# A layer of three branches on one core: half of one branch's projection moved ahead, and two branches of the merge in turn

## The chip, the cores and the metric

The kernel runs on one core of a Trainium2 chip. The metric is the device time of one execution in microseconds (us); three runs of the kernel before gave 1663.97, 1666.6 and 1668.9 us, with a median of 1666.6.

## What is computed

One layer of a flow-matching backbone works on 1024 latent tokens of width 1024 (and 256 context tokens). Three branches of width 512 run on one input projection: 0, a Hyena branch of two long convolutions; 1, a two-dimensional transform in groups of channels; 2, a bidirectional mLSTM. The part of the reference that the change touches merges them:

```python
ys = jnp.stack([y_hy, y_fn, y_ml], axis=2)
proj = jnp.einsum("blkc,kcd->blkd", ys, lp["w_branch"])
g = jax.nn.sigmoid(gate_pre).reshape(B, L, N_BRANCH, D_MODEL)
return jnp.sum(g * proj, axis=2) @ lp["w_out"]
```

A mixture-of-experts part and a final norm follow. Everything is float32.

## The kernel before

All is held with channels on the 128 partitions and the 1024 tokens along a row. A float32 product is made of three: both operands are split into a high part, rounded by a cast on ScalarE (ACT), and the low rest, a subtraction on VectorE (DVE) or GpSimd (POOL) (`split`, L213; `parts`, L223), and `mm3` (L228) multiplies high by high, high by low and low by high into one PSUM tile. Loads go through SyncE's queue (SP) (`load`, L218).

The order of the parts: the input projection, the mLSTM and the transform branch, whose results lie in DRAM (`yd[2]`, `yd[1]`) long before they are used; the last gates (`gate`, L830; the last one by `proj_last`, L766, whose evacuations, `rest`, come in the next stage); the Hyena convolutions (`stage_conv`, L1144); the merge (`stage_merge`, L1509); the output projection (`stage_out`, L1552).

The convolutions run in four passes (order and half of the channels; L1158), each of eight blocks j (even or odd frequencies `par`, part `fb`). A block takes a forward product into a bank of PSUM tag `gp` (two), multiplies it with the filter `kk` on VectorE (L1057, L1059), splits the result, and, two blocks later, adds the inverse product to the tiles `acc` (`conv_inv`, L1062): four per half pass, six banks in all. `conv_in` (L993) makes the next pass's input by transposes; `conv_out` (L1096) makes a pass's output, and in passes 2 and 3 sends it from the tiles `f` to `yd[0]`. Matrices come through `mat` (L969) and four buffers `ms`. At the start, `rest` is ordered behind the cast of the last of three forward matrices (L1155).

The merge runs over the branches 2, 1, 0 (n = 0, 1, 2; L1521). For each it loads four y tiles of 128x1024 through two buffers (`GA` `y`) and splits them, then makes eight groups d: a weight block of 128x512 (split by ACT and POOL, three buffers), a gate tile `g`, 24 products (two halves of 512 tokens, four parts k, three products each) into `pb` (four tiles, all eight banks), and VectorE's gate multiplication; from n = 1 on, POOL adds to `acc`. Branch 1 prepares the parts of `w_out` beside its groups. Branch 1's y tiles have a place of their own, GY; those of branches 2 and 0 share one (`y0` to `y3` in GN and G, one buffer each).

What sets the order: each engine runs its instructions in an order that a scheduler draws up when the program is built, from the order of the source, its priorities and its idea of the durations; it may put an instruction whose operands come later behind another. Tiles live in pools that are laid out like stacks from two sides of SBUF, so that a new pool lies where closed ones were, and a tile waits for the tiles that lay in its place. On the left side T (18 tiles of 4 KB, the projection's input) and then P (`w`, three of 4 KB, `wh`, `wl` and `z`, two of 4 KB each, in this order) are followed by C1 (56 KB) and CN (24 KB), and these by MT, WO and GN (112 KB). On the right, CA, C and CT (24, 48 and 20 KB) are followed by GA, G, GT and GY, of which GY (32 KB) covers CT and the last output's tiles `u` and `f` in it, and some tiles of C.

Of the kernel before, what the change touches and what calls it, by code (L numbers as in the profile page):

```python
# [8 lines left out]
F32 = mybir.dt.float32  # L9
F32R = mybir.dt.float32r  # L10
I32 = mybir.dt.int32
AF = mybir.ActivationFunctionType
ALU = mybir.AluOpType
# [4 lines left out]
L = 1024  # L18
# [146 lines left out]
class Prog:  # L165
# [22 lines left out]
        self.n += 1  # L188
        return self.dp.tile(list(shape), dt, name=f"{name}_{self.n}", tag=f"{name}_{self.n}")

    PSB = {"gp": 2, "q": 2, "b1": 2, "pb": 1, "acc": 6, "ph": 8}

    def ps(self, tag="pb", shape=(128, 1024)):
        self.n += 1
        pool = self.pg if tag == "gp" else self.pp
        return pool.tile(list(shape), F32, name=f"{tag}_{self.n}", tag=tag, bufs=self.PSB[tag])

    def psum(self, name):
# [4 lines left out]
        if name != "start":  # L203
            self.PSB = dict(self.PSB, pb=3)
        if name == "merge":
            self.pgc.__exit__(None, None, None)
        if name in ("merge", "moe"):
            self.PSB = dict(self.PSB, pb=4)
        self.ppc = self.tc.tile_pool(name=name, bufs=1, space=PSUM, reuse_waits="tile")
# [924 lines left out]
    def conv_first(self):  # L1134
# [6 lines left out]
        for kind in "fi":  # L1141
            self.mat(kind, 0, 0, 0)

    def stage_conv(self):  # L1144
        nc = self.nc
        self.pool("C1")
        self.pool("CN")
        self.psum("conv")
        blocks = [(par, fb) for par in range(2) for fb in range(4)]
        passes = [(o, half) for o in range(2) for half in range(2)]  # L1150
        ut, last, acc = {0: self.ut0}, [], {}
        for fb in (1, 2, 3):
            self.mat("f", 0, 0, fb)
        first = self.copied, self.lower
        with self.tc.issue_after(self.copied.ins):  # L1155
            for f in self.rest:
                f()
        for n, (o, half) in enumerate(passes):  # L1158
            acc[n] = {}
            for j, (par, fb) in enumerate(blocks):  # L1160
                for kind, i in (("f", j + FA), ("i", j - IA)):
                    if n == 0 and 0 <= i < 4:
                        self.mat(kind, 0, 0, i)
                if n == 0 and j < 4:
                    for k in range(2):
                        self.mat("o", 1, k, j)
                with ExitStack() as es:
                    for i in () if n or j else first:
                        es.enter_context(self.tc.issue_after(i.ins))
                    y = self.conv_fwd(ut[n], o, half, par, fb)  # L1170
                if len(last) == 2:
                    self.conv_inv(*last.pop(0))
                if j == 1 and n:
                    out = self.conv_out(acc[n - 1], *passes[n - 1])
                if n and j in (1, JA, JB):
                    next(out, None)
                last.append((acc[n], y, o, half, par, fb))
                if j == JC and n < 3:
                    ut[n + 1] = list(self.conv_in(self.xd[0], passes[n + 1][1], *((self.out_tiles,) if n else ())))
        for a in last:  # L1180
            self.conv_inv(*a)
        for _ in self.conv_out(acc[3], 1, 1):
            pass
        self.psum("merge")
        self.close("CN")
        self.close("C1")
        self.close("CT")
        self.close("C")
        self.close("CA")
        if "hy" in self.dbg:  # L1190
            nc.sync.dma_start(self.dbg["hy"], self.yd[0])
# [317 lines left out]
    def stage_merge(self):  # L1509
        nc = self.nc  # L1510
        A = self.A
        self.pool("GA", "right")
        self.pool("G", "right")
        self.pool("GT", "right")
        self.pool("GY", "right")
        self.pool("MT")
        self.pool("WO")
        self.pool("GN")
        self.acc = [self.t("MT", "acc", 2, F32, (128, 4, L)) for _ in range(2)]
        self.wo = []  # L1520
        for n, br in enumerate((2, 1, 0)):  # L1521
            yh, yl = [], []
            with self.tc.high_priority() if n == 0 else ExitStack():
                for ct in range(4):
                    pool, tag, bufs = ("GY", "y", 4) if n == 1 else ("GN" if ct < 2 else "G", f"y{ct}", 1)
                    h, l = self.parts(pool, tag, bufs, self.load("GA", "y", 2, self.yd[br, ct]))
                    yh.append(h), yl.append(l)
            for d in range(8):
                mh, ml = self.parts("GA", "m", 3, self.load("GA", "m", 2, A["w_br"][br, d], (128, 4, 128)), "g")
                g = self.t("GT", "g", 3)  # L1530
                nc.sync.dma_start(g, self.gd[br, d])
                p = self.ps("pb")
                acc = self.acc[d // 4][:, d % 4, :]
                for a in (0, 512):
                    for k in range(4):
                        self.mm3(p[:, a:a + 512], mh[:, k, :], ml[:, k, :], yh[k][:, a:a + 512], yl[k][:, a:a + 512],
                                 k == 0, k == 3)
                if n == 0:
                    nc.vector.scalar_tensor_tensor(acc, g, 1.0, p, op0=ALU.add, op1=ALU.mult)
                else:  # L1540
                    nc.vector.scalar_tensor_tensor(g, g, 1.0, p, op0=ALU.add, op1=ALU.mult)
                    (nc.vector if n == 2 and d > 5 else nc.gpsimd).tensor_add(acc, acc, g)
                if n == 1:
                    self.wo.append(self.parts("WO", "w", 8, self.load("GT", "w", 2, A["w_out"][d])))
        self.close("GY")
        self.close("GN")
        self.close("GT")
        self.close("G")
        self.close("GA")
# [707 lines left out]
```

## Time and profile before

| what | before |
|---|---|
| median of three runs | 1666.6 us |
| the profiled execution | 1659.17 us |
| its span in the trace | 1657.4 us |
| its granted TensorE clock (mean) | 0.971 |
| PE busy | 1552.4 us (94%) |
| VectorE busy | 1177.0 us (71%) |
| ScalarE busy | 684.7 us (41%) |
| GpSimd busy | 306.7 us (19%) |

The trace is that of one execution; its times are counted from the start of the span. PE is the matrix engine's products, PEld its weight loads, which overlap them. A product of an instruction line is shown with its duration from start to end; products are pipelined, so that the next one starts before. "Granted clock" is the share of full speed that TensorE got in a stretch. Lines of a helper (L215, L216, L220, L230 to L232) belong to many stages; they are told apart by the names of the tiles.

### The profile page before, as it was taken

What the parts mean: (1) busy time and instruction counts of PE and PEld (TensorE: products, weight loads), DVE (VectorE), ACT (ScalarE), POOL (GpSimd) and SP (SyncE); (2) the same over time, 40 slices, a digit from 0 to 9 for tenths busy, and PEclk for the clock granted to TensorE, in tenths of its full rate; (3) what the DMA queues carried; (4) which work ended last, traced back from release to release, by engine and by line L of the source; (5) the groups of instructions that cost most, each with busy time, mean ns of one, the idle gap of its engine ahead of it and who ended that gap; (6) DMA issues with size and microseconds to landing.
All of it is one profiled execution on the core that took longest, in us unless ns stands there. A gap on an engine that the chain in (4) does not pass through costs nothing. (4 is left out here: it accounts for less than half of the span.)

```text
span 1657.4 us, 22624 instructions
## 1 busy us (share of the span) xinstructions
PE 1552.4 (94%) x8489; PEld 1304.9 (79%) x8489; DVE 1177.0 (71%) x1766; ACT 684.7 (41%) x1050; POOL 306.7 (19%) x275
## 2 busy tenths in 40 slices
PE   6999999999999999899998899999999979999993
PEld 2678877788888887778886788888888779999992
DVE  3898775866786887788653999953255577777776
ACT  3566455433222124345424444332033354544553
POOL 0000000000000001000001000126623355565651
PEclk7999999999999999999999999999999979999997
DMA  7453666412332365877325433685462479999984
GB/s 287 142 193 138 217 227 224 161 67 83 105 121 76 127 236 189 285 266 277 136 103 173 160 96 107 220 312 182 152 247 103 143 253 243 322 301 284 265 229 177
DMA packets 125570, 315.97 MB, mean 191 GB/s; under 512 B 17689, under 2 KB 43281, under 8 KB 125458
## 3 DMA queue, kind: packets, MB, share of 16 engines
q1 hardware_dynamic: 113354, 279.77, 48.8%
q0 software_dynamic: 10496, 32.36, 8.2%
q10 hardware_dynamic: 1608, 2.37, 0.4%
q8 instruction: 68, 1.11, 0.3%
q14 instruction: 44, 0.36, 0.1%
HBM read 227.53 MB, written 86.91 MB: 190 GB/s over the span
## 5 line engine op out<-in xcount | busy, mean ns | idle before, releaser
L230 PE MATMUL gp<-ht,wh 128*128 128x512 f32 x768 | 303.1, 395 | 4.7 <-ACT wh L215 3.6
L232 PE MATMUL gp<-ht,wl 128*128 128x512 f32 x768 | 301.2, 392 | 0.9 <-DVE wl L216 0.9
L231 PE MATMUL gp<-ht,wh 128*128 128x512 f32 x768 | 301.5, 393 | 0.0
L230 PEld LDWEIGHTS gp<-ht,wh 128*128 128x128 f32 x768 | 144.5, 188 | 37.5 <-ACT wh L215 4.5
L232 PEld LDWEIGHTS gp<-ht,wl 128*128 128x128 f32 x768 | 144.5, 188 | 30.7 <-DVE wl L216 1.3
L231 PEld LDWEIGHTS gp<-ht,wh 128*128 128x128 f32 x768 | 144.6, 188 | 28.7 <-issue 0.2
L230 PE MATMUL pb<-xh,gh 128*128 128x224 f32 x512 | 142.8, 279 | 0.0
L232 PE MATMUL pb<-xh,gl 128*128 128x224 f32 x512 | 141.8, 277 | 0.0
L231 PE MATMUL pb<-xl,gh 128*128 128x224 f32 x512 | 141.7, 277 | 0.0
L801 DVE SCALAR_TENSOR_TENSOR u<-z,hy_cw,u 128x945 f32<-128x945 f32 (+2 forms) x96 | 117.3, 1221 | 13.3 <-ACT u L793 11.1
L216 DVE TENSOR_TENSOR wl<-w,wh 128x1024 fp32r<-128x1024 f32 x57 | 70.3, 1235 | 58.9 <-ACT wh L215 58.6
L215 ACT CAST wh<-w 128x1024 fp32r<-128x1024 f32 x57 | 59.8, 1050 | 122.2 <-PE gp L231 82.5
L230 PEld LDWEIGHTS pb<-xh,gh 128*128 128x128 f32 x512 | 99.4, 194 | 0.3 <-ACT xh L215 0.2
L231 PEld LDWEIGHTS pb<-xl,gh 128*128 128x128 f32 x512 | 99.5, 194 | 0.1
L232 PEld LDWEIGHTS pb<-xh,gl 128*128 128x128 f32 x512 | 99.5, 194 | 0.0
L801 DVE SCALAR_TENSOR_TENSOR u<-z,ml_cw,u 128x945 f32<-128x945 f32 (+2 forms) x64 | 77.9, 1220 | 27.4 <-ACT u L793 26.4
L786 ACT ACTIVATE z<-gp,b_cols 128x512 f32<-128x512 f32 x46 | 31.4, 685 | 137.1 <-PE gp L232 136.9
L216 POOL TENSOR_TENSOR ml<-m,mh 128x512 fp32r<-128x512 f32 x24 | 35.6, 1485 | 204.4 <-ACT mh L215 197.6
L949 POOL MEMSET z<- 128x1024 f32 x1 | 1.0, 958 | 358.5 <-DVE u L801 358.5
L786 ACT ACTIVATE z<-gp,bh 128x512 f32<-128x512 f32 x46 | 31.4, 683 | 73.9 <-PE gp L232 54.3
L1781 POOL DMA_INDIRECT sum<-y,sidx x26 | 47.3, 1820 | 71.4 <-DVE y L1896 68.0
L1815 DVE TENSOR_TENSOR gl<-x,gh 128x1024 fp32r<-128x1024 f32 x33 | 42.1, 1282 | 25.2 <-ACT gh L1813 23.8
(619 smaller groups left out, 3982.3 us busy)
## 6 DMA issues: line engine op xcount, KB each, us to landing
w<-in_ada_rest SPq DMA_DIRECT2D x32, 512.0 KB
w<-in_w_gu SPq DMA_DIRECT2D x32, 512.0 KB
x<-in_w_gu SPq DMA_DIRECT2D x32, 512.0 KB
w<-in_w_gate SPq DMA_DIRECT2D x24, 512.0 KB
g<-gd SPq DMA_DIRECT2D x24, 512.0 KB
gd<-z SPq DMA_DIRECT2D x23, 512.0 KB
r<-in_ada_in SPq DMA_DIRECT2D x16, 512.0 KB
pd<-ft SPq DMA_DIRECT2D x32, 256.0 KB
```

The source lines that it names most:

```text
L215: self.copied = nc.scalar.copy(hi, src)
L216: return (nc.vector if eng == "v" else nc.gpsimd).tensor_sub(lo, src, hi.bitcast(F32))
L230: mm(ps, lh, rh, start=start, stop=False)
L231: mm(ps, lh, rl, start=False, stop=False)
L232: mm(ps, ll, rh, start=False, stop=stop)
L786: return lambda s, p: self.nc.scalar.activation(z[:, s], p, func, bias=bias, scale=scale)
L801: last = nc.vector.scalar_tensor_tensor(ui[:, r0:r1, c0:c1], zi[:, r0 + dy:r1 + dy, c0 + dx:c1 + dx], taps[:, i:i + 1], ui[:, r0:r1, c0:c1 ...
L949: nc.gpsimd.memset(zt, 0.0)
L1781: return self.nc.gpsimd.indirect_dma_start(out=out, out_offset=bass.IndirectOffsetOnAxis(ap=ix, axis=0), in_=src, in_offset=None, **kw)
L1815: lo = (nc.vector if engines[i] == "v" else nc.gpsimd).tensor_sub(ml, m, mh.bitcast(F32))
```

## The change

A new pool CF and a generator `branch_first` are added to the convolutions. It loads tokens 0 to 511 of branch 2's four y tiles and, one after the other, its eight weight blocks (through the buffers `ms`), splits them on ACT and VectorE, and makes the products of these tokens, one step of three products at a time, into a PSUM tile `fl`; a finished block is copied to SBUF by ACT and written to DRAM as `bd`. `stage_conv` takes one step of it behind each block from pass 0, block 6, on, and one more in blocks 2 and 6; what is left comes behind the last output. `acc` has five banks instead of six, and `fl` the one.

In the merge, branch 2 loads, splits and multiplies tokens 512 to 1023 alone; VectorE takes the first half from `bd` and the second from PSUM. Its groups run in turn with those of branch 1 (2, 1, 2, 1, ...), whose y tiles are prepared before the first of them; branch 0 follows as before. `w_out` is prepared in every second group of branch 1 and the first four of branch 0.

```diff
-    PSB = {"gp": 2, "q": 2, "b1": 2, "pb": 1, "acc": 6, "ph": 8}
+    PSB = {"gp": 2, "q": 2, "b1": 2, "pb": 1, "acc": 5, "fl": 1, "ph": 8}
...
+    def branch_first(self):
+
+        nc = self.nc
+        self.bd = self.dram([8, 128, 512], name="bd")
+        ys = [self.parts("CF", "y", 4, self.load("CA", "ms", 4, self.yd[2, ct, :, :512], (128, 512))) for ct in range(4)]
+        weights = lambda d: self.parts("CF", "w", 2, self.load("CA", "ms", 4, self.A["w_br"][2, d], (128, 4, 128)))
+        ws = [weights(0)]
+        yield
+        for d in range(8):
+            mh, ml = ws.pop()
+            p = self.ps("fl", (128, 512))
+            for k in range(4):
+                self.mm3(p, mh[:, k, :], ml[:, k, :], *ys[k], k == 0, k == 3)
+                if k == 1 and d < 7:
+                    ws.append(weights(d + 1))
+                if k == 3:
+                    z = self.t("CF", "z", 2, F32, (128, 512))
+                    nc.scalar.copy(z, p)
+                    nc.sync.dma_start(self.bd[d], z)
+                yield
+
     def stage_conv(self):
         nc = self.nc
+        self.pool("CF")
         self.pool("C1")
         self.pool("CN")
...
+        fill = self.branch_first()
...
                     y = self.conv_fwd(ut[n], o, half, par, fb)
+                if (n, j) == (0, 4):
+                    next(fill)
+                if (n, j) > (0, 5):
+                    next(fill, None)
+                    if j % 4 == 2:
+                        next(fill, None)
                 if len(last) == 2:
...
         for _ in self.conv_out(acc[3], 1, 1):
             pass
+        for _ in fill:
+            pass
         self.psum("merge")
         self.close("CN")
         self.close("C1")
+        self.close("CF")
...
-        for n, br in enumerate((2, 1, 0)):
+        def prepare(n, br):
             yh, yl = [], []
+            f = 512 if n == 0 else 0
             with self.tc.high_priority() if n == 0 else ExitStack():
                 for ct in range(4):
                     pool, tag, bufs = ("GY", "y", 4) if n == 1 else ("GN" if ct < 2 else "G", f"y{ct}", 1)
-                    h, l = self.parts(pool, tag, bufs, self.load("GA", "y", 2, self.yd[br, ct]))
+                    y = self.load("GA", "y", 2, self.yd[br, ct, :, f:], (128, L - f))
+                    h, l = (self.t(pool, tag + x, bufs, F32R)[:, f:] for x in "hl")
+                    self.split(h, l, y)
                     yh.append(h), yl.append(l)
-            for d in range(8):
+            return f, yh, yl
+
+        def step(n, br, d, f, yh, yl):
+            if True:
                 mh, ml = self.parts("GA", "m", 3, self.load("GA", "m", 2, A["w_br"][br, d], (128, 4, 128)), "g")
                 g = self.t("GT", "g", 3)
                 nc.sync.dma_start(g, self.gd[br, d])
                 p = self.ps("pb")
                 acc = self.acc[d // 4][:, d % 4, :]
-                for a in (0, 512):
+                for a in (0, 512)[n == 0:]:
                     for k in range(4):
-                        self.mm3(p[:, a:a + 512], mh[:, k, :], ml[:, k, :], yh[k][:, a:a + 512], yl[k][:, a:a + 512],
-                                 k == 0, k == 3)
+                        s = slice(a - f, a - f + 512)
+                        self.mm3(p[:, a:a + 512], mh[:, k, :], ml[:, k, :], yh[k][:, s], yl[k][:, s], k == 0, k == 3)
                 if n == 0:
-                    nc.vector.scalar_tensor_tensor(acc, g, 1.0, p, op0=ALU.add, op1=ALU.mult)
+                    b = self.load("GT", "w", 2, self.bd[d], (128, 512))
+                    nc.vector.scalar_tensor_tensor(acc[:, :f], g[:, :f], 1.0, b, op0=ALU.add, op1=ALU.mult)
+                    nc.vector.scalar_tensor_tensor(acc[:, f:], g[:, f:], 1.0, p[:, f:], op0=ALU.add, op1=ALU.mult)
                 else:
                     nc.vector.scalar_tensor_tensor(g, g, 1.0, p, op0=ALU.add, op1=ALU.mult)
                     (nc.vector if n == 2 and d > 5 else nc.gpsimd).tensor_add(acc, acc, g)
-                if n == 1:
-                    self.wo.append(self.parts("WO", "w", 8, self.load("GT", "w", 2, A["w_out"][d])))
+                if n == 1 and d % 2 or n == 2 and d < 4:
+                    self.wo.append(self.parts("WO", "w", 8, self.load("GT", "w", 2, A["w_out"][len(self.wo)])))
+
+        y0, y1 = prepare(0, 2), prepare(1, 1)
+        for d in range(8):
+            step(0, 2, d, *y0)
+            step(1, 1, d, *y1)
+        y2 = prepare(2, 0)
+        for d in range(8):
+            step(2, 0, d, *y2)
         self.close("GY")
```

## Rows read from the trace of the kernel before

**Rows 1.** The page: span, busy time and share of the engines, and one group.

```profile
span 1657.4 us, 22624 instructions
PE 1552.4 (94%) x8489; PEld 1304.9 (79%) x8489; DVE 1177.0 (71%) x1766; ACT 684.7 (41%) x1050; POOL 306.7 (19%) x275
...
L230 PEld LDWEIGHTS gp<-ht,wh 128*128 128x128 f32 x768 | 144.5, 188 | 37.5 <-ACT wh L215 4.5
```

**Rows 2.** Passes 0 to 3, merge: length; busy PE, PEld, DVE, ACT, POOL; clock; DMA share.

```profile
905.90:938.50 32.60, 26.80 (x177) 23.97 (x176) 30.19 (x45) 17.36 (x34) 6.05 (x4) 0.90 0.58 194
938.50:980.80 42.30, 38.48 (x259) 34.97 (x258) 39.11 (x61) 17.30 (x34) 0.00 (x0) 0.96 0.32 100
980.80:1021.35 40.55, 36.66 (x257) 33.60 (x256) 39.20 (x61) 17.37 (x34) 0.00 (x0) 1.00 0.33 104
1021.35:1061.40 40.05, 37.45 (x257) 35.22 (x256) 38.37 (x54) 17.56 (x33) 4.64 (x3) 0.96 0.61 197
...
1072.60:1206.30 133.70, 132.94 (x587) 109.74 (x586) 58.93 (x55) 30.23 (x39) 66.03 (x56) 1.00 0.58 203
```

**Rows 3.** Timeline of PE, the merge's first and last product: start, us, what.

```profile
1072.61 0.39 PE L230 MATMUL pb<-y0h,mh 128*128 128x512 f32 x1
...
1204.01 0.39 PE L232 MATMUL pb<-y3h,ml 128*128 128x512 f32 x1
```

**Rows 4.** Timelines of ACT and PE at the start of the convolutions.

```profile
895.65 1.67 ACT L215 CAST nh<-ms 128x512 fp32r<-128x512 f32 x3 [1.90 <-PE gp L231]
903.35 1.37 ACT L786 ACTIVATE u<-gp,bh 128x512 f32<-128x512 f32 x2 [6.04 <-PE gp L232]
...
903.61 0.39 PE L232 MATMUL gp<-ht,wl 128*128 128x512 f32 x1
904.10 0.39 PE L230 MATMUL gp<-u2h,mh 128*128 128x256 f32 x1
```

**Rows 5.** Timeline of DVE, two low parts of 128x512 and the next start.

```profile
1033.03 1.29 DVE L216 TENSOR_TENSOR u1l<-raw,u1h 128x512 fp32r<-128x512 f32 x2
1034.23 0.68 DVE L216 TENSOR_TENSOR yl<-t,yh 128x512 fp32r<-128x512 f32 x1
```

**Rows 6.** Busy time in one stretch of pass 0, columns as in rows 2.

```profile
920.00:930.00 10.00, 8.16 (x48) 7.54 (x47) 8.04 (x16) 2.56 (x5) 0.00 (x0) 0.68 0.43 157
```

**Rows 7.** Timelines of SP and ACT, the y tiles of branch 1 and the last output.

```profile
1075.32 1.46 SPq L220 DMA_DIRECT2D y<-yd  x2
...
1088.83 1.46 SPq L220 DMA_DIRECT2D y<-yd  x2
...
1080.80 0.33 ACTq L1128 DMA_DIRECT2D yd<-f  x1
...
1093.08 1.05 ACT L215 CAST yh<-y 128x1024 fp32r<-128x1024 f32 x1 [2.11 <-DMA y<-yd]
1094.58 1.05 ACT L215 CAST yh<-y 128x1024 fp32r<-128x1024 f32 x1 [0.45 <-DMA y<-yd]
```

**Rows 8.** Timeline of PE at the start of the merge; in brackets, the wait.

```profile
1074.19 0.39 PE L230 MATMUL pb<-y0h,mh 128*128 128x512 f32 x1
1075.35 0.50 PE L231 MATMUL pb<-y2l,mh 128*128 128x512 f32 x1 [0.76 <-DVE y2l L216]
```

**Rows 9.** Groups of PE in pass 2, by form; then two 256-column products of the timeline.

```profile
L230 PE MATMUL acc<-mh,yh 128*128 128x512 f32 x16 | 6.3, 393 | 0.0
L231 PE MATMUL acc<-ml,yh 128*128 128x512 f32 x15 | 5.9, 393 | 0.0
L232 PE MATMUL acc<-mh,yl 128*128 128x512 f32 x15 | 5.7, 389 | 0.0
...
904.55 0.28 PE L230 MATMUL gp<-u2h,mh 128*128 128x256 f32 x1
904.67 0.28 PE L231 MATMUL gp<-u2l,mh 128*128 128x256 f32 x1
```

**Rows 10.** Waits of PE from 900 to 1075: us in total, times, longest.

```profile
PE acc L230 <- ACT yh L215: 8.7, 6, 2.6
```

## The prediction

> **What bounds the kernel now.** I read the page first: TensorE is busy in 94% of the span [rows 1], so only a stage where it is not can give anything. Then busy time by stretch [rows 2]. The four convolution passes (L1158) and their tail run from 905.9 to 1072.6 us, the merge (L1521) from there to 1204. In the merge PE is busy for 132.94 of 133.70 us while VectorE has little to do; in passes 1 to 3 VectorE is busy for 39.11 of 42.30, 39.20 of 40.55 and 38.37 of 40.05 us, and PE is idle for 3.82, 3.89 and 2.60 us, 10.3 together. So the merge is bound by products, the convolutions by VectorE with PE close behind. The timeline of PE gives the price of a product: 576 products of 512 columns (24 groups of 24) start between 1072.61 and 1204.01 us [rows 3], and take until 1204.24 with the last; 131.6 us, of which 0.76 is one wait [rows 8]: 0.227 us each. The 390 ns that a line shows for one overlap their neighbours.
>
> **The change, part by part.**
>
> Removed from the merge: half of each group of branch 2, 8 x 12 = 96 products x 0.227 = **-21.8 us**, all on the path, since PE has no other idle time there. They come back in the convolutions as 32 steps of three products (0.68 us each): three in pass 0, ten in pass 1, ten in pass 2, nine in pass 3. What counts is how much of that fits into idle time.
>
> Start of the convolutions. The pools lie behind one another: CF takes 28 KB (ys 16, weights 8, z 4), so C1 and CN begin 28 KB higher. CN was in the last tiles of T and the first of P; it now covers P from its 12th KB to its 36th, which is wh, wl and z. The last gate's weights are read until its last product (903.61, 0.39 long [rows 4]). Two of the three forward matrices find room in the weights of the gate before; the third cast of nh (in before at 895.65, three in 1.67 us) must wait until 904.0. The evacuations of that gate stand behind this cast by order (L1155), and the first convolution's PSUM bank is one of those that they empty. So: cast until 904.6, evacuation (half of 1.37 us) until 905.3, first product at 905.4 instead of 904.10: **+1.3 us**. Bounds: 0, if the allocator finds another place, and 3 if both evacuations count.
>
> Pass 0. VectorE gets the low parts of four ys and of two weights, 6 x 0.60 us (from start to start of such operations [rows 5]) = 3.6 us. It is idle for 1.96 us between 920 and 930 [rows 6], where the ys land. **+1.6 us**; bounds 0 and 3.6. The six casts more on ACT, which is busy for 17.36 of 32.60 us [rows 2], I count at nothing: ACT waits for VectorE there; without this cover it would be up to 0.7 us each, as two evacuations took 1.37 [rows 4].
>
> Passes 1 to 3. 29 steps x 0.68 = 19.7 us of PE work come in. Against that stand 10.3 us of idle time, and 3.3 us lost to the clock: passes 1 and 3 had a granted clock of 0.96 [rows 2], that is 4% of 42.3 and of 40.05 us, as in 920 to 930 (0.68 [rows 6]) where products ran partly at the lower of the two levels, 1.2 instead of 2.4 GHz, after PE had waited. I let 1.0 us of idle time per pass remain, for the waits that no step can fill. So 19.7 - (10.3 - 3.0) - 3.3 = **+9.1 us**. Lower bound 6.1 (nothing remains), upper 19.7 (nothing fits, no clock comes back). VectorE is no second bound: six weights more at 0.60 less what two y splits of half the width save, 0.6 each, is +2.4 us on 116.7, against 132 us that these passes then take. The sixth bank of acc that goes away costs at most one evacuation more per pass, and stands in the 1.0. Eight small writes of bd and twelve loads join SP's queue; a write waits for its evacuation on ACT, and the next loads of kk stand behind it. In passes 1 and 2 the DMA share is 0.32 and 0.33 [rows 2], and kk has three buffers; nothing counted.
>
> Sum of the convolutions: 1.3 + 1.6 + 9.1 = **+12.0 us**.
>
> Start of the merge. T is the end of the last convolution (1072.61 in before). Branch 1's four y tiles are needed behind one half group (2.7 us) now, not behind eight whole ones (43.6 us). The two buffers of y that bring them come free when branch 2's last low parts are done: in before the first pair is issued at 1075.32, T + 2.7, the second at 1088.83, and its casts run at 1093.08 and 1094.58 [rows 7], 4.3 and 5.8 us behind their issue. They also need the places of the last u, f and t of the convolution; the last output leaves f at 1080.80 [rows 7], T + 8.2. So in the changed kernel: first pair split by about T + 10.5 (2.7, the later landing of 5.8, a cast of 1.05 and a low part of about 1.2, twice the 0.60 of half the width [rows 5]), second by about T + 18.5. For PE there are meanwhile (PE's order is made beforehand, and mixes groups where an operand is late: a product of the second group ran ahead of one that waited for y2l, [rows 8]): groups 0 and 1 of branch 2 (5.4 us), group 2 when its weights are split again (2.7), and the halves of two groups of branch 1 that need the first pair only (5.4), 13.5 us in all; three weight buffers allow no more. That leaves 5.0 us of waits where before had 0.76: **+4.2 us**. Lower bound 0 (the order finds enough), upper 17.8 (rival 3). Two halves instead of one multiply-add for branch 2, and loading the stored half, cost nothing: VectorE is busy for 58.93 of 133.70 us there [rows 2], and PE does not read them; without that cover, one operation of 0.6 us a group.
>
> Start of branch 0. Its y tiles now take places that branch 2 reads until one group before, instead of nine groups before. Cover: that group (5.4 us) and the first halves of the next two (5.4). Need: casts and low parts of a pair (3.3 us), load of the second pair (4.3 to 5.8), 2.2 more: 9.8 to 11.3. **0**, upper bound 3. w_out's last parts are made four groups before the end; nobody waits.
>
> Sum: 12.0 - 21.8 + 4.2 = **-5.6 us**. The profiled execution took 1659.17 us (span 1657.4, 1.8 around it); this gives 1653.6. It is 7.4 us below the median of the runs, 1666.6, to which I apply the same difference: **1661.0 us**. About 0.3% (5 us) is what a measurement of this kernel can tell from no change.
>
> **A rule that gives another result.** In pass 2 PE's products are busy for 36.66 of 40.55 us and its weight loads for 33.60 [rows 2]. The Trainium skill (Perfetto Trace Analysis, section Identifying the Most-Contended Engine) says that the busy share of matmuls is a bad measure of TensorE's room, since they are pipelined, and to go by the busy share of the weight loads. By it, room would be 7 us in a pass, not 3.9, and the sum that of rival 1.
>
> **Rivals.**
> 1. *PE has more room than its busy time shows*, as much as its weight loads leave. Ten steps are 30 loads x 0.188 us [rows 1] = 5.6, less than the 6.95 us in which loads are idle [rows 2]. Then VectorE alone sets the passes: +2.4 instead of +9.1, and -12.3 in all: **1654.3**. Against it: of the 257 operations of pass 2, 46 have 512 columns (0.227 us each), and the other 211, nearly all of 256 columns, are 0.12 us apart from start to start [rows 9]: 10.4 + 25.3 = 35.7, almost the whole busy time of 36.66.
> 2. *The steps go in series*: PE's idle time is waits on VectorE and ACT, and an order made beforehand puts the steps beside it. For it: at the start PE waits in front of single products of acc for yh (8.7 us in six waits over the stage [rows 10]). Then +19.7 instead of +9.1: 22.6 - 21.8 + 4.2 = +5.0, **1671.6**. That the products are not moved at all, because the order puts them behind the last convolution, comes to the same.
> 3. *Slower: branch 1's y chain takes the place of the wait removed.* Place: PE, behind the second half group. If the chain keeps the pace of before, second pair ready at T + 24 (last cast done at 1095.6 [rows 7], and 1.2 for the low part), and PE's order has only groups 0 and 1 ahead of it, it waits 24 - 5.4 = 18.6 us, 17.8 more than before: 12.0 - 21.8 + 17.8 = +8.0, **1674.6**. It decides the sign from 10.6 us of waits on, and makes the kernel measurably slower from 15.6. Against it: in before nothing hurried this chain.
>
> **How the numbers follow.** Forecast 0.52, with a range of its own of 1656 to 1667 (idle time left 0 to 2 us per pass, waits 2 to 8); rival 1 0.17, rival 2 0.17, rival 3 0.14. Faster by over 0.3%: rival 1 and three fifths of the forecast, 0.48. Slower: most of rival 3, half of rival 2, 0.21. Within: the rest, 0.31. The range reaches down past rival 1 (idle time and waits at their low bounds take it to 1651) and up to rival 2 with a little more waiting: 1651 to 1673.
>
> **What would show it.** In the profile after: conv passes of about 43 to 45 us with PE's idle time near 1; first convolution product 1.3 us after the last gate's product; the merge 17 to 18 us shorter; and in it a few us of waits of PE for yh or yl of branch 1. Wrong if VectorE has gaps and PE none (rival 1), passes that grow by 6.8 us (rival 2), or one wait over 10 us early in the merge (rival 3).

## The result: slower by 1.1%

The changed kernel takes **1683.4 us** (median of three runs, 1682.18 to 1690.42) against 1666.6: ratio 1.011, 95% interval 1.0091 to 1.0128. The forecast was 1661.0. The profiled execution after took 1690.42 us (span 1688.6), 7.0 above its median, where before's lay 7.4 below its own; so stages are compared here, not spans. What lies behind the merge took 451 to 462 us in the profiled executions of this study, with no edit there.

First the page, then busy time by pass (to the first eviction, where VectorE takes a pass's sums from PSUM), tail and merge, in the columns of [rows 2]:

```profile
span 1688.6 us, 22721 instructions
PE 1562.5 (93%) x8489; PEld 1309.2 (78%) x8489; DVE 1193.4 (71%) x1786; ACT 694.5 (41%) x1070; POOL 304.7 (18%) x275
```

```profile
907.00:947.40 40.40, 32.00 (x199) 28.05 (x200) 34.13 (x50) 23.76 (x44) 8.31 (x6) 0.87 0.78 245
947.40:988.76 41.36, 41.35 (x281) 37.85 (x280) 40.57 (x63) 19.03 (x37) 0.00 (x0) 1.00 0.40 127
988.76:1036.56 47.80, 45.05 (x288) 40.77 (x287) 41.31 (x64) 20.75 (x40) 0.00 (x0) 0.96 0.35 105
1036.56:1075.66 39.10, 39.10 (x266) 36.23 (x265) 33.73 (x50) 15.89 (x32) 3.76 (x3) 1.00 0.57 178
1075.66:1092.00 16.34, 15.59 (x81) 12.94 (x81) 12.08 (x20) 4.92 (x11) 0.57 (x1) 1.00 0.37 123
1092.00:1231.40 139.40, 117.73 (x481) 94.00 (x480) 66.05 (x61) 30.01 (x39) 69.17 (x53) 0.90 0.62 217
```

The number of products is the same (x8489). Passes 1 and 3 are now full of them, PE busy for 41.35 of 41.36 and 39.10 of 39.10 us. But pass 0 is longer, with the DMA share up from 0.58 to 0.78, and in the merge PE, which had 0.76 us to spare, is idle for 21.7 us and the clock is 0.90. To compare all runs I take three marks from PE's timeline: the last gate product, the end of the last convolution product (T), and the first product of the output stage. **Convolutions** (first mark to T) and **merge** (T to the third) are then 168.8 and 131.6 us before, 187.3 and 139.5 after: +18.5 and +7.9. Single profiled executions scatter: where the convolutions' instructions are those of before they took 167.2 to 171.2 us (before, e2, e6 and e8 below), and 180.7 to 184.0 in three runs that share another form of them (e4, e5, e9). A difference of 3 to 4 us between two such numbers says nothing by itself.

The waits of PE inside the merge, from its timeline, with the product ahead of the first:

```profile
1094.62 0.39 PE L232 MATMUL pb<-y3h,ml 128*128 128x512 f32 x1
1101.62 0.79 PE L230 MATMUL pb<-yh,mh 128*128 128x512 f32 x1 [6.62 <-ACT yh L215]
...
1109.19 0.80 PE L231 MATMUL pb<-yl,mh 128*128 128x512 f32 x1 [5.49 <-DVE yl L216]
1118.32 0.50 PE L231 MATMUL pb<-yl,mh 128*128 128x512 f32 x1 [0.82 <-DVE yl L216]
...
1175.89 0.50 PE L231 MATMUL pb<-y0l,mh 128*128 128x512 f32 x1 [0.62 <-DVE y0l L216]
1179.20 0.50 PE L231 MATMUL pb<-y1l,mh 128*128 128x512 f32 x1 [2.35 <-DVE y1l L216]
1183.97 0.80 PE L230 MATMUL pb<-y2h,mh 128*128 128x512 f32 x1 [4.04 <-ACT y2h L215]
1190.04 0.66 PE L231 MATMUL pb<-y3l,mh 128*128 128x512 f32 x1 [1.73 <-DVE y3l L216]
```

The first three waits (12.9 us) are for branch 1's y tiles, the last four (8.7) for branch 0's. PE's order has branch 1's first product right behind the first half group (1094.62); before the second wait ends, at T + 17.2, PE has made 16 products, 3.6 us of work. Who was late for the first shows in the timelines of ACT, DVE and SP:

```profile
1100.53 1.04 ACT L215 CAST yh<-y 128x1024 fp32r<-128x1024 f32 x1 [5.05 <-DVE f L1126]
...
1105.67 0.69 DVE L1578 SCALAR_TENSOR_TENSOR acc<-g,w 128x512 f32<-128x512 f32 x1 [4.35 <-DMA w<-bd]
1107.91 2.36 DVE L216 TENSOR_TENSOR yl<-y,yh 128x1024 fp32r<-128x1024 f32 x2 [1.54 <-DMA g<-gd]
...
1109.16 1.45 SPq L220 DMA_DIRECT2D y<-yd  x2
```

ACT issues the writes of the last outputs and stands there until VectorE has made them (f); the cast of branch 1's first y is behind them. Then VectorE, which takes its work in order, stands 4.35 us at the multiply-add of a stored half that is still being loaded, and the low part that PE wants is behind it. The second pair of y is issued at T + 17.2, where before it was T + 16.2 [rows 7]: the chain keeps its old pace, and eight whole groups no longer cover it. In and behind these waits PE has the lower of its two clock levels, 1.2 instead of 2.4 GHz (granted clock 0.50):

```profile
1102.00:1112.00 10.00, 4.51 (x11) 3.00 (x11) 4.28 (x4) 2.09 (x2) 0.00 (x0) 0.50 0.83 320
```

The 480 products at 0.227 us are 109.0 us and the waits 21.7; the other 8.8 of 139.5 are this clock (what the starts of the products lie further apart than 0.227 us, waits left out, adds up to 8.6). At the other end of the stage, SP issues the loads of branch 0's second pair when the low parts of the first free their buffers, in the middle of the products that want both (DVE, SP):

```profile
1176.35 2.79 DVE L216 TENSOR_TENSOR y1l<-y,y1h 128x1024 fp32r<-128x1024 f32 x1
...
1178.46 1.03 SPq L220 DMA_DIRECT2D y<-yd  x2
```

### The profile page after: what moved, and what is told of

The parts are those of the page before. It is cut to its first block, busy times and chain, and to the rows that moved or that the text cites. A ratio compares the mean times of both kernels' runs of the same rounds, so it can differ in the third digit from the quotient of the medians.

```text
span 1688.6 us, 22721 instructions
## 1 busy us (share of the span) xinstructions
PE 1562.5 (93%) x8489; PEld 1309.2 (78%) x8489; DVE 1193.4 (71%) x1786; ACT 694.5 (41%) x1070; POOL 304.7 (18%) x275
## 4 chain that ended last, share of the span: by engine, by line
PE 68%; DVE 12%; DMA 10%; issue 5%; ACT 3%; POOL 1%; SPq 0%; POOLq 0%; ACTq 0%; DVEq 0%
PE gp L230 11%; PE gp L231 11%; PE gp L232 10%; PE pb L231 7%; PE pb L230 7%; PE pb L232 6%; PE ph L230 2%; PE ph L232 2%; PE ph L231 2%; PE pb L1879 1%; PE q L355 1%; PE acc L230 1%; DMA ow<-od 1%; PE pb L1485 1%; DMA g<-gd 1%
## 5 line engine op out<-in xcount | busy, mean ns | idle before, releaser
L230 PEld LDWEIGHTS gp<-ht,wh 128*128 128x128 f32 x768 | 144.8, 189 | 37.3 <-ACT wh L215 4.4
L232 PEld LDWEIGHTS gp<-ht,wl 128*128 128x128 f32 x768 | 144.6, 188 | 30.8 <-DVE wl L216 1.3
L801 DVE SCALAR_TENSOR_TENSOR u<-z,ml_cw,u 128x945 f32<-128x945 f32 (+2 forms) x64 | 78.0, 1221 | 27.4 <-ACT u L793 26.4
```

The costliest lines, as they stand in the source:

```text
L230: mm(ps, lh, rh, start=start, stop=False)
L232: mm(ps, ll, rh, start=False, stop=stop)
L801: last = nc.vector.scalar_tensor_tensor(ui[:, r0:r1, c0:c1], zi[:, r0 + dy:r1 + dy, c0 + dx:c1 + dx], taps[:, i:i + 1], ui[:, r0:r1, c0:c1 ...
```

## The experiments

Ratios are to the kernel before in the same job (its medians there 1669.1 to 1671.9 us); stage times are those of each profiled execution.

In what follows "the fill" is branch 2's first halves, made in the convolutions, and "the turn" the order 2, 1, 2, 1 of the merge.

**The two parts apart, and the bank.** e1 has the fill and the half groups, with the merge in the order 2, 1, 0 of before:

```diff
-        y0, y1 = prepare(0, 2), prepare(1, 1)
...
+        for n, br in enumerate((2, 1, 0)):
+            y = prepare(n, br)
+            for d in range(8):
+                step(n, br, d, *y)
```

> Half of branch 2's products in the convolutions, as in the change, but the merge in the order of before (branch 2's half groups, then branch 1, then branch 0). Theory A (the turn of the two branches costs the time: waits of PE for y tiles, 21.7 us by the trace, and products at the lower clock behind them): the convolutions grow by some 18 us, the merge loses the 21.8 us of products and little else, so -4 to +5 us against before, 1662 to 1672. Theory B (the products in the convolutions cost the time, the turn is cheap): at least +12 us, 1679 or more.

e2 has the turn alone: convolutions of before, no stored halves, full groups (`for a in (0, 512)`, f = 0).

> Whole groups of branch 2 in the merge, no products in the convolutions, but branches 2 and 1 in turn, as in the change. Theory A: the waits stay, shorter by the 2.7 us that a whole first group covers more: +15 to +27 us against before, 1682 to 1694. Theory B: less than +5 us.

e3 is before with five banks for acc, the sixth unused.

```diff
-    PSB = {"gp": 2, "q": 2, "b1": 2, "pb": 1, "acc": 6, "ph": 8}
+    PSB = {"gp": 2, "q": 2, "b1": 2, "pb": 1, "acc": 5, "ph": 8}
```

> The kernel before with five banks for acc instead of six, nothing else. If the missing bank is what lengthens the convolutions: +6 us or more. If the products do it: 0 to +2 us, and passes of about 41 us as before.

| run | ratio (95%) | convolutions | merge | PE's waits in the merge |
|---|---|---|---|---|
| before | 1 | 168.8 | 131.6 | 0.8 |
| after | 1.011 (1.0091 to 1.0128) | 187.3 | 139.5 | 21.7 |
| e1 fill | 1.0069 (1.0046 to 1.0092) | 185.7 | 130.3 | 13.7 |
| e2 turn | 1.0074 (1.0053 to 1.0095) | 167.9 | 144.6 | 10.2 |
| e3 bank | 1.0012 (0.9993 to 1.0032) | 172.3 | 131.7 | 0.8 |

Both parts cost, and nearly add up: in convolutions and merge together 15.6 us (e1) and 12.1 (e2) against 26.4 of the whole. By the medians e1 is 12.0 us slower than before, the number of its theory B, and e2 13.1, between its two. The bank is not told from nothing. e1 says most: 96 products gone from the merge bring **1.3 us**, not 21.8; its longest wait there, 8.0 us, is for weights. e2's cost is mostly one wait and the lower clock behind it, in the timelines of SP and PE:

```profile
1091.63 1.46 SPq L220 DMA_DIRECT2D y<-yd  x2
...
1089.36 0.80 PE L230 MATMUL pb<-yh,mh 128*128 128x512 f32 x1 [7.63 <-ACT yh L215]
```

**The place of the new pool.** e4 is e1 with CF opened last and closed first, so that C1 and CN lie where they did.

```diff
-        self.pool("CF")
         self.pool("C1")
         self.pool("CN")
+        self.pool("CF")
```

> As e1, with the pool CF opened behind C1 and CN, so that the first matrices lie where they lay before. If the start of the convolutions waits for the place of the third forward matrix (2.15 us of PE's wait, and 3 us of products at the lower clock, by the trace): 2 to 4 us less than e1, and the first convolution product within 0.3 us of the last gate's. If not: as e1.

Ratio 1.0054 (1.0034 to 1.0075), convolutions 180.9, merge 130.1. The first convolution product comes 0.49 us behind the last gate product, as before, where after had this (ACT, then PE):

```profile
904.71 1.66 ACT L215 CAST nh<-ms 128x512 fp32r<-128x512 f32 x3 [10.01 <-PE gp L231]
906.27 1.26 ACT L786 ACTIVATE u<-gp,bh 128x512 f32<-128x512 f32 x2
...
904.47 0.39 PE L232 MATMUL gp<-ht,wl 128*128 128x512 f32 x1
907.00 0.58 PE L230 MATMUL gp<-u2h,mh 128*128 128x256 f32 x1 [2.15 <-ACT u L786]
```

So the chain that I had worked out from the pools' places is there: cast, evacuation, product, and it costs 2.0 us at the mark (2.53 instead of 0.49). All three casts stand in it, where I had counted the third alone. Up to the first eviction of pass 0 e4 is 4.2 us shorter than e1 (39.3 instead of 43.5 us behind the last gate product); the ratios of the two are not told apart.

**What the merge can give back.** e5 is e4 with the stored halves loaded straight into the sum, past the two small buffers that VectorE frees; e8 leaves the first halves of branch 2 out, in the convolutions and in the merge.

```diff
-                    b = self.load("GT", "w", 2, self.bd[d], (128, 512))
-                    nc.vector.scalar_tensor_tensor(acc[:, :f], g[:, :f], 1.0, b, op0=ALU.add, op1=ALU.mult)
+                    nc.vector.scalar_tensor_tensor(acc[:, :f], g[:, :f], 1.0, acc[:, :f], op0=ALU.add, op1=ALU.mult)
...
+            for d in range(8) if n == 0 else ():
+                nc.sync.dma_start(self.acc[d // 4][:, d % 4, :512], self.bd[d])
```

> The fill alone with its pool last (e4), and the stored halves loaded straight into the sum's first halves, eight loads at the head of the merge, in place of eight loads through two small buffers. Queue theory: in e4 the sync queue stood behind the loads of the stored halves, whose two buffers VectorE gives free, and with it the weights and y of branch 1; then PE's waits in the merge fall from 12.7 us to under 4, the merge from 130.1 to 112 to 118 us, and the ratio to before from 1.005 to about 0.997. Rival, bytes: the same bytes still have to come in the same stretch (DMA share 0.9 to 1.02 there in e4), so the merge stays at 126 to 130 us and the ratio at 1.003 or more.

> Before with the first halves of the third branch's products left out altogether: nothing in the convolutions, nothing stored or loaded for them (their place in the sum takes a product of the gate with itself). It shows what the merge can give back at most with half groups in the order of before. Queue theory: without the stored halves' loads the merge falls by 16 us or more, to 110 to 116 us, ratio about 0.989. Rival: branch 1's y chain and the loads of gates and weights are the floor by themselves: the merge stays at 120 us or more, and only 12 us or less come back, ratio 0.993 or more.

e5: 1.008 (1.0049 to 1.011), merge 131.1, waits 13.4. My queue theory falls: past the small buffers nothing changes. e8: 0.996 (0.9938 to 0.9981), merge 124.7, waits 9.0. With nothing to load for the fill, 21.8 us less of products give 6.9 us; of the 14.9 that do not come back, 8.2 are waits and 6.7 the clock behind them. Its first 20 us of merge, busy time in the columns of [rows 2]; the operation of VectorE that ends the last output, SP's loads and PE's wait; and what SP's queue itself waited for longest:

```profile
1079.80:1084.80 5.00, 5.00 (x23) 3.90 (x23) 5.00 (x9) 1.25 (x2) 1.37 (x1) 1.00 0.00 0
1084.80:1089.80 5.00, 5.00 (x24) 4.14 (x23) 4.97 (x6) 0.70 (x2) 3.65 (x2) 1.00 0.61 224
1089.80:1094.80 5.00, 5.00 (x24) 4.14 (x23) 3.81 (x6) 2.64 (x3) 1.54 (x1) 1.00 1.02 382
1094.80:1099.80 5.00, 1.68 (x8) 1.06 (x6) 5.00 (x8) 0.38 (x1) 0.00 (x0) 1.00 0.97 357
...
1085.63 3.37 DVE L1126 TENSOR_TENSOR f<-u,f 128x512 f32<-128x512 f32 x2
...
1086.78 0.33 SPq L220 DMA_DIRECT2D m<-in_w_br  x1
...
1090.23 3.22 SPq L1558 DMA_DIRECT2D g<-gd  x3
1093.55 0.38 SPq L220 DMA_DIRECT2D m<-in_w_br  x1
...
1100.09 0.50 PE L230 MATMUL pb<-y0h,mh 128*128 128x512 f32 x1 [3.61 <-ACT mh L215]
...
SPq L220 <- POOL ml L216: 15.2, 1, 15.2
```

The DMA engines stand still at first (0.00), since SP's queue stands for 15.2 us, up to T + 6.9, at a load of weights whose buffer comes free when POOL has made a low part; that in turn waits for the place that PE's first half group gives back. The gates behind it wait for VectorE, which makes the convolutions' last outputs for 9 us behind T, so that the weights of the seventh half group are issued only at 1093.55, with the DMA engines full. PE does six half groups, and waits for them. Before's eight whole groups, 43.6 us, covered all of this.

**The turn, later.** e6 is e2 with four groups of branch 2 ahead of the turn, and four of branch 1 behind it; `w_out` is prepared with the groups of branch 1, as in before (in both traces its parts are made before branch 0 starts).

```diff
-        for d in range(8):
-            step(0, 2, d, *y0)
-            step(1, 1, d, *y1)
+        for d in range(4):
+            step(0, 2, d, *y0)
+        for d in range(4):
+            step(1, 1, d, *y1)
+            step(0, 2, d + 4, *y0)
+        for d in range(4, 8):
+            step(1, 1, d, *y1)
```

> The turn alone with full groups (e2), but begun after four groups of branch 2, so that four groups of branch 1 are left alone at its end. Theory: e2's cost is that the first group of branch 1 stands in PE's order before its y can be there, and that in turn branch 2's y tiles come free only one group ahead of branch 0; begun four groups later both are covered: PE's waits in the merge fall from 10.2 us to under 2, the merge from 144.6 to 131 to 134 us, ratio 1.000 to 1.002. Rival: the order in turn costs by itself (gate tiles, sums on POOL, loads of w_out): the merge stays above 138 us and the ratio at 1.005 or more.

1.0003 (0.9978 to 1.0029), merge 133.4, waits 1.5: the theory holds for the start. The turn costs nothing by itself; its start did. Its other end costs little alone: in e2, where branch 2's tiles come free as late as in after, PE waits for 0.8 us at the start of branch 0.

**The fill, later.** e7 is e5 with another pace of the parts.

```diff
-                if (n, j) == (0, 4):
+                if (n, j) == (0, 7):
                     next(fill)
-                if (n, j) > (0, 5):
+                if n:
                     next(fill, None)
-                    if j % 4 == 2:
+                    if j % 3 == 2:
                         next(fill, None)
```

> e5 with the fill begun at the last block of pass 0 instead of the fifth, its 32 parts spread over passes 1 to 3. Theory: e4's 4.4 us in pass 0 are the fill's loads ahead of the next pass's input on the sync queue and its casts, which ScalarE takes in order; begun late, pass 0 is back at 35 to 36 us (last gate product to first eviction; 34.9 before), the passes after it gain some 2 us for the 9 products moved there, and the run is 2 us or more below e5. Rival: the loads and casts cost the same wherever they stand: pass 0 shorter, pass 1 longer by as much, within 1 us of e5.

1.0022 (1.0005 to 1.0039); convolutions 176.8 us instead of 184.0, of which 1.4 are two of the 32 parts that now run behind T; merge 132.3. Only 2.2 us of the 7.2 come from pass 0 (last gate to first eviction 37.3, 39.5 in e5, 34.9 before): it is not back where the theory had it. That much is more than scatter: with the early fill of e4, e5 and e9 pass 0 took 39.3 to 40.1 us by these marks, with the late one of e7 and e10 to e12 36.2 to 37.3, and 33.2 to 34.9 where there is none (before, e2, e6, e8). Most, 6.7, comes from passes 1 to 3 (121.5 instead of 128.2), which neither theory expected; the tail gives 1.7 back. These 5.0 us are not told from scatter: passes and tail took 140.6 to 144.5 us in e4, e5 and e9, whose convolutions are the same. Passes 1 to 3 in e7:

```profile
944.46:988.65 44.19, 44.06 (x289) 39.69 (x288) 42.86 (x67) 20.11 (x40) 0.00 (x0) 1.00 0.48 148
988.65:1030.34 41.69, 41.60 (x280) 37.95 (x279) 40.53 (x63) 19.25 (x38) 0.00 (x0) 1.00 0.38 116
1030.34:1065.95 35.61, 35.61 (x237) 32.75 (x236) 33.26 (x51) 13.79 (x27) 0.00 (x0) 1.00 0.47 142
```

PE is full in all three, where after's pass 2 has a wait of 2.65 us for an evacuation and a clock of 0.96. What the early fill did to pass 0, in after's timelines of SP, ACT and PE:

```profile
922.91 0.80 SPq L220 DMA_DIRECT2D ms<-yd  x2
923.75 0.43 SPq L1001 DMA_DIRECT2D u<-xd  x1
...
926.15 0.42 SPq L1001 DMA_DIRECT2D u<-xd  x1
...
930.16 1.28 ACT L215 CAST yh<-ms 128x512 fp32r<-128x512 f32 x2 [2.85 <-DMA ms<-yd]
...
934.76 0.30 PE L1023 MATMUL gp<-ident,f 128*128 128x128 f32 x1 [1.74 <-DVE f L1013]
```

and in before's timeline of SP:

```profile
916.84 0.91 SPq L1001 DMA_DIRECT2D u<-xd  x2
```

The next pass's input stands among the four ys. It is issued 19.3 us behind the last gate product where before it was 13.2, the second half 21.7 instead of 13.7 (2.0 us of either are the later start); PE waits for what is made of it, and ACT stands in order at casts whose data are not there. How much of pass 0 is this order and how much the bytes (DMA share 0.78) is not separated.

**Loads ahead.** In e9 (e5's fill), e10 and e11 (a late fill that ends within pass 3) branch 2's gates and weights are loaded into the tiles of w_out, which are free until branch 1: all eight groups, or in e11 those behind the third.

```diff
+                for d in range(8):
+                    m, g = (self.t("WO", "w" + x, 8, F32R).bitcast(F32) for x in "lh")
```

> e5 with branch 2's gates and weights (eight of each) and the stored halves loaded at the head of the merge into tiles that stand free there (those of the output weights, written only from branch 1 on), in place of three gate tiles and two weight tiles that VectorE and POOL give back. Theory: in e8 the DMA engines stood idle for the first 5 us of the merge (share 0.00) and then ran full for 20 us, since VectorE, busy with the last outputs to 9 us after the last convolution product, gives no gate tile back; loads that wait for no engine start at the merge's head: PE's waits in the merge fall from 13.4 us to 3 to 6, the merge from 131 to 115 to 120 us, ratio to before 0.998 to 1.001 with the convolutions of e5 (184 us). Rival: it is branch 1's last outputs (VectorE to 9 us, write, load, cast) and the bytes that decide: the waits stay at 9 us or more, the merge at 124 us or more, ratio 1.003 or more.

> e9 with the fill begun at the last block of pass 0 and two parts at every other block, so that it ends in the middle of pass 3 (e7 began there, but ended behind the last pass and left branch 2's own y late). Theory: e7's shorter convolutions (176.8 us) and e9's shorter merge add up: conv and merge together 176 to 180 and 115 to 120 us, 3 to 8 us below before's 300.4, ratio 0.995 to 0.998. Rival: the parts cost passes 2 and 3 what pass 0 gains, or the merge's floor holds: ratio 1.000 or more.

> e10 with the first three groups' gates and weights again in the small tiles of before, filled ahead of the merge, and only groups 4 to 8 loaded early into the output weights' tiles. Theory: e10's wait of 10.6 us is the first weights, whose tiles come free only with the last convolution product; three groups (8.2 us of products) cover the loads that start there: PE's waits in the merge 3 to 6 us, the merge 115 to 119 us, with e10's convolutions (179.7) some 3 to 5 us under before, ratio 0.997 to 0.999. Rival: the bytes decide (share 1.0 for 30 us in e10), so the wait only moves to the fourth group: the merge stays at 122 us or more, ratio 1.001 or more.

| run | ratio (95%) | convolutions | merge | waits in the merge |
|---|---|---|---|---|
| e9 | 1.0029 (1.0011 to 1.0047) | 180.7 | 127.4 | 13.8 |
| e10 | 1.0028 (1.0008 to 1.0047) | 179.7 | 124.6 | 12.0 |
| e11 | 1.0021 (0.9996 to 1.0047) | 183.3 | 124.4 | 9.7 |

All three miss, and the numbers are those of the rivals: the wait goes to the first weights (10.2 us in e9, where their load is issued 3.2 us behind the end of the convolutions) or spreads over several (e11), and the merge comes to e8's 124.7 and no further. Gates and weights that wait for no engine do not remove this floor; which of the bytes and the chain of branch 1 holds it up, these three do not separate.

**Half the fill.** e12 moves only as much as the cover allows: the last four groups of branch 2, in 16 parts, one a block, in passes 1 and 2; the merge begins with four whole groups, in the order 2, 1, 0, with e5's loads and e4's pools.

```diff
+                if n:
+                    next(fill, None)
...
-        for d in range(8):
+        for d in range(4, 8):
             mh, ml = ws.pop()
...
-                for a in (0, 512)[n == 0:]:
+                for a in (0, 512)[n == 0 and d > 3:]:
```

> Half the fill: only the last four groups of branch 2 leave their first halves to the convolutions, in 16 parts, one a block, in passes 1 and 2; the merge begins with four full groups, and the order 2, 1, 0 stays. Theory: the full groups cover branch 1's last outputs and the loads as before's eight did, so that the 48 products (10.9 us) come back whole: merge 120 to 123 us with waits under 3, convolutions 171 to 174 us (168.8 in before), conv and merge 291 to 297 against 300.4, ratio 0.995 to 0.998. Rival: the floor of the merge (e8's 124.7 us with nothing to load for the fill) holds here too: merge 126 us or more, ratio 1.000 or more.

**0.9957** (0.993 to 0.9983), median 1661.37: faster than both (by 0.4% than before). Convolutions 172.7 (+3.9), merge 122.1 (-9.5 for 10.9 removed), as expected; convolutions and merge together 294.8 against 300.4. PE's waits in the merge and the output stage's start are down to this:

```profile
PE pb L232 <- POOL ml L216: 0.8, 1, 0.8
PE pb L231 <- DVE y2l L216: 0.8, 1, 0.8
PE ph L230 <- ACT mh L1676: 0.6, 1, 0.6
PE ph L232 <- DVE ml L1677: 0.4, 1, 0.4
```

## Why the prediction was wrong

Step by step, by the terms of its sum (marks as above; pass 0 ends at the first eviction):

| term | predicted | measured |
|---|---|---|
| start of the convolutions | +1.3 | +2.0 |
| pass 0 | +1.6 | +6.0 |
| passes 1 to 3 and tail | +9.1 | +10.4 |
| products gone from the merge | -21.8 | -21.8 |
| waits at the start of the merge | +4.2 | +12.2 |
| start of branch 0 | 0 | +8.7 |
| clock after these waits | not counted | +8.8 |

**The start of the merge** is the step that failed first. I let PE's order find 13.5 us of products beside the chain of branch 1's y, and let that chain run some 5 us faster than in before, because nothing had hurried it there. Neither came. PE's order put branch 1 behind the first half group, and 3.6 us of products were made by T + 17.2; the second pair was issued only then, and its last low part released PE at 1118.32, T + 26.4, where I had T + 18.5. What sets its pace is VectorE's work on the last outputs, and then a queue of loads that I had costed at nothing ("VectorE is busy for 58.93 of 133.70 us"): a share over the whole stage, where the first 30 us decide. This is the mechanism of rival 3, with 12.9 us of waits where it said 18.6. In the order of before it is weights that come late instead: e8 shows it without any of the fill's own loads, and of 21.8 us 6.9 come back.

**The start of branch 0** failed by the same kind of step. I counted 10.8 us of cover against 9.8 to 11.3 of need, and wrote 0; the bound of 3 was too small as well. The short cover alone is not it, since e2 has the same and waits for 0.8 us there. What I had left out stands under "w_out's last parts are made four groups before the end; nobody waits". In after ACT stands at a part of `w_out` that is still being loaded, with the casts of branch 0's y behind it; in e2 the cast follows as soon as PE gives the tile back (ACT, after and then e2):

```profile
1171.28 1.05 ACT L215 CAST wh<-w 128x1024 fp32r<-128x1024 f32 x1 [3.98 <-DMA w<-in_w_out]
...
1172.76 1.05 ACT L215 CAST y0h<-y 128x1024 fp32r<-128x1024 f32 x1
...
1167.01 1.05 ACT L215 CAST y0h<-y 128x1024 fp32r<-128x1024 f32 x1 [2.96 <-PE pb L232]
```

Branch 2's last products with this tile start at 1166.72 in after and at 1166.13 in e2, so after's cast is some 5 us late; then VectorE does work for `w_out` and branch 1 between the low parts. In e2 the loads of `w_out` are all issued by 1112.65, in after up to 1189.35; they share two buffers with the stored halves there. That these buffers hold them back was not tested apart.

**The clock** was in my reading of passes 1 and 3, but I put no price on it behind the new waits: 8.8 us, as much as branch 0's waits.

**Pass 0**: I counted VectorE's low parts and let ACT's casts and SP's loads pass at nothing, because ACT "waits for VectorE there". With an order made beforehand, a cast that waits for its load holds up those behind it, and u<-xd was a queue entry that I had not looked at. With the fill begun behind it (e7, e10 to e12) pass 0 is some 3 us shorter than with the early one, e7 2.2 us shorter than e5. About 2 more go with the place of the pool (e4 against e1, without the start); what is left over before, some 2 us, stays open.

**Right**: the start of the convolutions, with its chain (e4), was 0.7 us short; passes and tail took in 29 steps for 10.4 us, near the 9.1 (the difference is within the scatter), by idle time that filled and clock that came back. One by one the passes are not the 43 to 45 us that I had named: 41.4, 47.8 and 39.1, with 5.1 us more in the tail. So the sum is better than its parts. Rival 1 falls: passes 1 and 3 have PE busy to the last 0.01 us, and counted by their starts (0.227, 0.12 and 0.11 us apart for 512, 256 and 128 columns) the products of pass 1 fill 40.6 of its 41.36 us. Their weight loads are busy for 37.85 of 41.36 us in pass 1, so that by the rule of the Trainium skill (Perfetto Trace Analysis, section Identifying the Most-Contended Engine) 3.5 us would still be free; no wait of PE stands there and its starts leave 0.8 us, so the trace does not agree. Rival 2 falls too: the passes and the tail grew by 10.4 us, not by 19.7.

## What to carry to other kernels

A product taken from a stage where PE is always busy saves its time only as long as something else does not set the stage's start: look at what the removed work covered (here the last outputs of the stage before, their write, load and cast, and the refill of small buffers), and move only as much as leaves that cover, as e12 did with half. Read the busy share of queues and engines in the first microseconds of the stage, not over the whole of it. Where two branches are put in turn, look at both ends: the first group that needs the later branch's data, and what else stands in each engine's order when the branch behind needs its own.

## What was not expected of the hardware

A wait of PE cost more than itself here. Behind the 7.63 us in e2 the products start 0.43 us apart instead of 0.227 for 5 us more (granted clock 0.50, the lower level, from 1085 to 1095), and after's merge lost 8.8 us beside 21.7 of waits. And the DMA engines can be idle and too slow in one stretch: in e8's merge they moved nothing for 5 us, then 357 to 382 GB/s at a share near 1.0, and PE's wait for weights began 12 us behind the idle stretch.
